# The first phase of a two-layer decoder trunk, issued in an order written by hand

## The chip, the cores and the metric

The kernel runs on one core of a Trainium2 chip. The metric is device time in microseconds (us) of one execution of the whole program. The kernel before was timed three times; one more execution was recorded by the hardware profiler, and every row below comes from that one.

## What is computed

The reference is a decoder trunk of two layers on 256 tokens of width 2048 in float32. In each layer a conditioning vector c gives shift, scale and gate vectors (the ada vectors), which modulate the input of a mixer and of a SwiGLU network. Layer 0 mixes with forgetting attention and, in parallel, an S5 state-space layer. Layer 1 has sliding-window attention. What matters here is the beginning of layer 0:

```python
mod = silu(c) @ w_ada[layer] + b_ada[layer]
sh1, sc1, g1, sh2, sc2, g2 = split(mod, 6)
h = x * (1 + sc1) + sh1
proj = h @ w_in          # q, k, v, forget logits f, and u, the input of S5
```

The S5 layer also needs parameters that depend on no token: powers of exp(lambda dt), sine and cosine tables, and products of these with the input and output matrices b and c.

## The kernel before

Everything is held transposed, with features on the 128 partitions and the 256 tokens along the free dimension. The width of 2048 makes 16 tiles of 128 features (`KT` = 16). A float32 weight tile is multiplied in three parts. `split` (lines 257 to 263) rounds a stretch of weights to a high half `wh` on ScalarE (the cast L261) and takes the rest as `wl` on VectorE (L262). The input is split likewise into `hi` and `lo`, side by side in `hp`. `mm3` (lines 602 to 605) then issues wh x hi (L603), wh x lo (L604) and wl x hi (L605), 256 columns each, for each tile of 128 x 128.

**The first phase** (lines 611 to 676) runs over the 16 input tiles k. For each k it computes the shift and scale of these 128 features, modulates x, and adds the products with 12 of the 32 output tiles of `w_in` (the 8 of u and 4 of k) into six PSUM banks. A step k has these parts:

- the *ada matmuls* L650: four pieces of `ada_s` against silu(c), 16 matmuls in the source and 32 records in the trace, into the bank `abank`;
- the copy of their partial sums to SBUF, L654 on ScalarE;
- two matmuls with `sel4` that add up these sums, L656 (four records);
- the *modulation*: L658 (adds the bias) and L660 (x times scale plus shift) on VectorE, L661 (`hi`) on ScalarE, L662 (`lo`) on VectorE;
- for each of two halves hf: `split` of 6 weight tiles, and the products, 18 matmuls.

Between these parts, `adv()` advances a generator, `s5_params` (lines 369 to 518), by one chunk up to its next `yield`. Its first five chunks are chains of VectorE instructions on 128 x 32 elements. Four chunks follow with three VectorE instructions on 128 x 512 (L460 to L464) and three ScalarE ones (L465 to L467), then eight chunks of three VectorE instructions (L475 to L481). Then, for each of four quarters, come two chunks of three VectorE instructions, the second with four ScalarE ones (L501), four groups of four transposes on TensorE (L506) each with a copy on ScalarE (L507), and 32 small matmuls into the bank `kc` (L514), whose copy (L518) opens the next chunk. Before, the four transpose groups of a quarter make two pieces. `make_crow` (lines 319 to 325) spreads silu(c) over the partitions, 8 matmul records in a call, four calls in steps 1 to 4.

**What sets the order.** The program is written once in Python, and a scheduler orders each engine's instructions as it finds them ready in its own timing, with dependences kept; each engine then runs its queue in that order. A few instructions are kept in their written order among themselves: the loads on SP, and the splits (`front`, lines 250 to 251).

**Transfers.** The weights come through a ring of `RING` = 9 tiles of 512 KB, on the queue of SP. Piece n + 9 can be issued when piece n was read (`release_piece`, lines 246 to 248). The pieces of the first phase are listed in the order in which they are sent (lines 614 to 618): four of ada_s and two of w_s (384 KB each) for each k. Three other loads are issued in the loop (`early`, line 622): the rest of the first half of x in step 0, the S5 arrays in step 1, the second half of x in step 4. `wh` and `wl` have three buffers each. After the phase, lines 677 to 696 compute the forget logits, finish the generator and copy the banks out; all other products follow from a planned stream of pieces.

Of the kernel before, what the change touches and what calls it, by code (L numbers as in the profile page):

```python
# [19 lines left out]
KT = D // 128  # L20
# [11 lines left out]
EK = (1, 4, 1, 2)  # L32
# [12 lines left out]
def _start_tiles():  # L45
    return [AB_U + i for i in range(8)] + [AB_K + i for i in range(4)]
# [219 lines left out]
def build(tc, I, out):  # L266
    nc = tc.nc
    V, A, PE, G = nc.vector, nc.scalar, nc.tensor, nc.gpsimd

    with ExitStack() as es:  # L270
        c = Ctx(tc, I, out, es)
# [47 lines left out]
        def make_crow(g):  # L319
            b = c.px.tile([128, 512], F32, tag="aux3", name=c.name("cr"))  # L320
            for i in range(4):
                k = 4 * g + i
                PE.matmul(b[:, 128 * i:128 * i + 128], lhsT=cs[:, k:k + 1].to_broadcast([128, 128]), rhs=ident,
                          start=True, stop=True, skip_group_check=True)
            A.copy(crow[:, 512 * g:512 * g + 512], b)
# [43 lines left out]
        def s5_params():  # L369
# [116 lines left out]
            for qd in range(4):  # L486
                H = slice(128 * qd, 128 * qd + 128)
                br, bi = (x[:, H].rearrange("p (a o h) -> p a o h", o=1, h=16).to_broadcast([128, 8, 4, 16]) for x in (b_re, b_im))
                wr, wi = (x[:, :, 8 * qd:8 * qd + 8].rearrange("p s (a o) -> p a s o", o=1).to_broadcast([128, 8, 4, 16])
                          for x in (wvr, wvi))  # L490
                e4 = [x.rearrange("p (a s h) -> p a s h", a=8, s=4) for x in (er, ei, w1, w2)]
                V.tensor_tensor(e4[0], br, wr, ALU.mult)
                V.tensor_tensor(e4[2], bi, wi, ALU.mult)
                V.tensor_tensor(er, er, w1, ALU.subtract)
                yield
                V.tensor_tensor(e4[1], bi, wr, ALU.mult)
                V.tensor_tensor(e4[3], br, wi, ALU.mult)
                V.tensor_tensor(ei, ei, w2, ALU.add)
                for cc, e in ((0, er), (1, ei)):
                    for g in range(2):  # L500
                        A.activation(eb[:, cc, :, g, :], a3(e), AF.Copy, scale=m2[:, g:g + 1])  # L501
                yield
                for aa in range(4):
                    b = c.px.tile([128, 512], F32, tag="aux3", name=c.name("tr"))
                    for n in range(4):
                        PE.transpose(b[:, 128 * n:128 * n + 128], ebf[:, n % 2, 2 * aa + n // 2, :], ident)  # L506
                    A.copy(el[qd][:, 512 * aa:512 * aa + 512], b)  # L507
                    if aa == 1:
                        yield
                b = c.px.tile([128, 512], F32, tag="aux3", name=c.name("kc"))  # L510
                for i in range(4):
                    for jj in range(2):
                        for cc in range(2):
                            PE.matmul(b[32 * i:32 * i + 32, 64 * jj:64 * jj + 64], lhsT=ebf[:, cc, 4 * jj + i, 96:128],  # L514
                                      rhs=gcv[cc][:, :, 8 * qd + 4 * jj + i, :], start=(cc == 0), stop=(cc == 1),
                                      skip_group_check=True, tile_position=(0, 32 * i))
                yield
                V.tensor_copy(kc[:, H], b[:, 0:128])  # L518
# [83 lines left out]
        def mm3(dst, wh, wl, P, k, first, last):  # L602
            PE.matmul(dst, lhsT=wh, rhs=hi_of(P, k), start=first, stop=False, skip_group_check=True)  # L603
            PE.matmul(dst, lhsT=wh, rhs=lo_of(P, k), start=False, stop=False, skip_group_check=True)  # L604
            PE.matmul(dst, lhsT=wl, rhs=hi_of(P, k), start=False, stop=last, skip_group_check=True)  # L605
# [5 lines left out]
        hp = pair_of(0, 1, 2, 3)  # L611

        n_st = len(_start_tiles())
        for k in range(KT):
            for q in range(4):
                c.add_piece(I["ada_s"][4 * k + q], 1024)
            for q in range(2):
                c.add_piece(I["w_s"][2 * k + q], 64 * n_st)
        stream_items = make_items(c, I)

        c.dma_to(RING - 1)
        early = {0: lambda: c.load(x_lo[:, 2 * T:], I["xT"][0][:, 2 * T:]), EK[0]: s5_load,
                 EK[1]: lambda: c.load(x_hi, I["xT"][1])}

        c.free_aux = deque()
        ubank = [c.acc() for _ in range(4)]
        kbank = [c.px.tile([128, 512], F32, tag=f"aux{i}", name=c.name("kb")) for i in range(2)]
        abank = c.px.tile([128, 512], F32, tag="aux2", name=c.name("ab"))
        ada0 = [scr[:, 256 * i:256 * i + 256] for i in range(2)]
# [8 lines left out]
        def adv():  # L638
            try:
                next(s5job)  # L640
            except StopIteration:
                pass

        for k in range(KT):
            early.get(k, lambda: None)()
            for q in range(4):
                t = c.ptiles[6 * k + q]
                for j in range(4):
                    kk = 4 * q + j
                    PE.matmul(abank[32 * j:32 * j + 32, 0:256], lhsT=cs[:, kk:kk + 32], rhs=t[:, 256 * j:256 * j + 256],  # L650
                              start=(q == 0), stop=(q == 3), skip_group_check=True, tile_position=(0, 32 * j))
                c.release_piece(6 * k + q)
            a = ada0[k % 2]
            A.copy(a, abank[:, 0:256])  # L654
            for v in range(2):
                PE.matmul(abank[:, 256 + 2 * k + v:257 + 2 * k + v], lhsT=a[:, 128 * v:128 * v + 128],  # L656
                          rhs=sel4, start=False, stop=True, skip_group_check=True)
            V.tensor_tensor(m0v[:, k, :], abank[:, 256 + 2 * k:258 + 2 * k], b0v[:, k, :], ALU.add)  # L658
            xt = xs[k // 8][:, k % 8, :]
            V.tensor_scalar(xt, xt, m0v[:, k, 1:2], m0v[:, k, 0:1], op0=ALU.mult, op1=ALU.add)  # L660
            A.copy(hi_of(hp, k), xt)  # L661
            V.tensor_sub(lo_of(hp, k), xt, hi_of(hp, k).bitcast(F32))  # L662
            for hf in range(2):
                hw = 64 * n_st
                wh, wl = c.split(c.ptiles[6 * k + 4 + hf][:, 0:hw], hw)
                c.release_piece(6 * k + 4 + hf)
                for i in range(n_st // 2):
                    s = hf * (n_st // 2) + i
                    bk = ubank[s // 2] if s < 8 else kbank[(s - 8) // 2]
                    o = bk[:, 256 * (s % 2):256 * (s % 2) + 256]  # L670
                    W = slice(128 * i, 128 * i + 128)
                    mm3(o, wh[:, W], wl[:, W], hp, k, k == 0 and s % 2 == 0, k == KT - 1)
            if EK[2] <= k < EK[2] + 4:
                make_crow(k - EK[2])
            for _ in range(EK[3]):
                adv()
        fbank = c.px.tile([128, 512], F32, tag="aux2", name=c.name("fb"))
        for k in range(KT):
# [968 lines left out]
```

## Time and profile before

| | |
|---|---|
| time, median of 3 runs | 2296.44 us (2294.65 to 2297.05) |
| the profiled execution | 2297.39 us |
| its span, first to last instruction | 2295.5 us |
| granted TensorE clock, mean | 0.989 of 2.4 GHz |
| TensorE matmuls (PE) busy | 2230.2 us, 97% |
| VectorE (DVE) busy | 1728.8 us, 75% |
| ScalarE (ACT) busy | 1133.3 us, 49% |
| HBM read | 576.55 MB, 252 GB/s over the span |

PE stands for TensorE's matmuls, PEld for its weight loads, which overlap them, DVE for VectorE, ACT for ScalarE and SP for the engine whose queue issues the weight transfers. A row of the timeline has the start and the duration in us, the engine, the source line, the operation, output <- input, and in brackets how long the engine stood idle before it and what ended that. A duration includes the tail of an instruction, which overlaps the next one; the distance between starts is the pace.

### The profile page before, as it was taken

Reading aid. Unit: us, or ns where it says so; the run is one execution under the profiler, and the core shown is the slowest. Engines: PE = TensorE matmul, PEld = TensorE weight load, DVE = VectorE, ACT = ScalarE, POOL = GpSimd, SP = SyncE. Lnnn points to the kernel's source line nnn. Section 1 sums busy time; section 2 is a strip of 40 time slices with the busy share of each in tenths; the row PEclk is TensorE's granted clock in tenths of the full one; section 3 lists DMA queues with packets and bytes.
Section 4 is the critical chain, followed back from the end, with each engine's and each line's share of the span. In section 5 each row is a group of like instructions: output and inputs, shape, how many; then the busy total and the mean of one; then the engine's idle time right before and its main releaser. Section 6 shows DMA issues by size and latency. Waiting matters only on the chain.

```text
span 2295.5 us, 38210 instructions
## 1 busy us (share of the span) xinstructions
PE 2230.2 (97%) x14702; PEld 1941.1 (85%) x14702; DVE 1728.8 (75%) x3062; ACT 1133.3 (49%) x1816; POOL 2.3 (0%) x6
## 2 busy tenths in 40 slices
PE   6999999999999999999999999999999999999996
PEld 4778887889888888888888988889888888888885
DVE  6648887888888888888887988687777555555576
ACT  3456565365444334444445665466444434444444
POOL 0000000000000000000000000000000000000000
PEclk9999999999999999999999999999999999999998
DMA  8998787948999999888875865357887666665662
GB/s 320 353 335 324 275 307 267 332 158 297 321 319 318 317 324 317 316 318 319 317 234 150 299 220 180 120 156 254 270 272 250 186 188 187 186 190 186 191 185 73
DMA packets 161479, 581.16 MB, mean 253 GB/s; under 512 B 18320, under 2 KB 18960, under 8 KB 160912
## 3 DMA queue, kind: packets, MB, share of 16 engines
q1 hardware_dynamic: 159984, 575.49, 73.4%
q10 hardware_dynamic: 1312, 3.23, 0.4%
q8 instruction: 115, 1.88, 0.3%
q14 instruction: 68, 0.56, 0.1%
HBM read 576.55 MB, written 2.10 MB: 252 GB/s over the span
## 4 chain that ended last, share of the span: by engine, by line
PE 95%; DVE 2%; ACT 1%; DMA 1%; issue 0%; ACTq 0%; DVEq 0%
PE acc L608 43%; PE acc L609 22%; PE acc L603 6%; PE acc L604 6%; PE acc L605 6%; PE acc L1291 2%; PE ab L650 1%; PE aux L556 1%; PE aux L727 1%; PE aux L1137 1%; PE aux L1125 0%; PE aux L1110 0%; PE aux L805 0%; PE aux L1109 0%; ACT wh L261 0%; DVE wl L262 0%
## 5 line engine op out<-in xcount | busy, mean ns | idle before, releaser
L608 PE MATMUL acc<-hp,wh 128*128 128x512 f32 x4288 | 1492.5, 397 | 3.6 <-DVE z L943 2.5
L609 PE MATMUL acc<-hp,wl 128*128 128x256 f32 x4288 | 1170.2, 280 | 0.5 <-DVE wl L262 0.5
L262 DVE TENSOR_TENSOR wl<-w,wh 128x1024 fp32r<-128x1024 f32 (+1 forms) x712 | 862.7, 1212 | 405.8 <-ACT wh L261 392.6
L261 ACT CAST wh<-w 128x1024 fp32r<-128x1024 f32 (+1 forms) x712 | 740.4, 1041 | 853.4 <-PE acc L608 459.5
L608 PEld LDWEIGHTS acc<-hp,wh 128*128 128x128 f32 x4288 | 792.8, 188 | 184.5 <-ACT lnb L963 2.8
L609 PEld LDWEIGHTS acc<-hp,wl 128*128 128x128 f32 x4288 | 808.8, 189 | 19.4 <-DVE wl L262 2.0
L534 DVE CUSTOM_DVE_ANT_0 w<-w,crow 128x1024 f32<-128x1024 f32 x280 | 341.1, 1220 | 0.0
L603 PE MATMUL acc<-hp,wh 128*128 128x256 f32 x1120 | 312.0, 294 | 19.9 <-ACT hp L1036 13.2
L604 PE MATMUL acc<-hp,wh 128*128 128x256 f32 x1120 | 318.9, 291 | 0.7 <-DVE hp L662 0.7
L605 PE MATMUL acc<-hp,wl 128*128 128x256 f32 x1120 | 303.4, 290 | 0.0
L603 PEld LDWEIGHTS acc<-hp,wh 128*128 128x128 f32 x1120 | 213.3, 196 | 36.5 <-ACT hp L1036 14.4
L604 PEld LDWEIGHTS acc<-hp,wh 128*128 128x128 f32 x1120 | 218.8, 195 | 8.1 <-issue 5.4
L605 PEld LDWEIGHTS acc<-hp,wl 128*128 128x128 f32 x1120 | 210.7, 195 | 3.4 <-issue 3.0
L943 DVE SCALAR_TENSOR_TENSOR z<-acc,mod,z 128x256 f32<-128x256 f32 x180 | 85.9, 482 | 37.0 <-PE acc L609 33.9
L1213 ACT COPY ftmp<-acc 128x256 f32<-128x256 f32 x80 | 29.8, 373 | 116.7 <-PE acc L609 116.7
L1214 DVE TENSOR_TENSOR ftmp<-acc,ftmp 128x256 f32<-128x256 f32 x80 | 33.9, 423 | 27.8 <-ACT ftmp L1213 27.8
L650 PE MATMUL ab<-w,cs 128*32 128x256 f32 x512 | 36.5, 403 | 14.9 <-ACT cs L315 11.7
L1291 PE MATMUL acc<-wh,hp 128*128 128x512 f32 (+1 forms) x192 | 47.5, 357 | 0.0
L1291 PEld LDWEIGHTS acc<-wh,hp 128*128 128x128 f32 x192 | 33.9, 189 | 5.8 <-issue 0.8
L1218 DVE TENSOR_TENSOR ftmp<-ftmp 128x256 f32<-128x256 f32 x80 | 33.9, 423 | 4.7
L650 PEld LDWEIGHTS ab<-w,cs 128*32 128x32 f32 x512 | 15.6, 113 | 25.3 <-ACT cs L315 11.7
L1225 DVE TENSOR_TENSOR hp<-ftmp,hp 128x256 fp32r<-128x256 f32 x88 | 36.6, 420 | 0.1
(302 smaller groups left out, 1451.8 us busy)
## 6 DMA issues: line engine op xcount, KB each, us to landing
w<-in_w_gu SPq DMA_DIRECT2D x352, 512.0 KB, 4.4
w<-in_ada SPq DMA_DIRECT2D x320, 512.0 KB, 4.9
w<-in_w_dn SPq DMA_DIRECT2D x176, 512.0 KB, 4.4
w<-in_ada_s SPq DMA_DIRECT2D x64, 512.0 KB, 6.2
w<-in_w_ab SPq DMA_DIRECT2D x40, 512.0 KB, 6.0
w<-in_w_c SPq DMA_DIRECT2D x40, 512.0 KB, 4.3
w<-in_w_oab SPq DMA_DIRECT2D x32, 512.0 KB, 5.0
w<-in_w_oc SPq DMA_DIRECT2D x32, 512.0 KB, 3.8
```

What stands on the lines that cost most here:

```text
L261: self.front(nc.scalar.copy(wh[:, :n], src), "act")
L262: self.front(nc.vector.tensor_sub(wl[:, :n], src, wh[:, :n].bitcast(F32)))
L534: c.front(V.tensor_tensor_reduce(t, t, crow[:, 1024 * half:1024 * half + 1024], scale=1.0, scalar=0.0, op0=ALU.mult, op1=ALU.add, accum_ou ...
L603: PE.matmul(dst, lhsT=wh, rhs=hi_of(P, k), start=first, stop=False, skip_group_check=True)
L604: PE.matmul(dst, lhsT=wh, rhs=lo_of(P, k), start=False, stop=False, skip_group_check=True)
L605: PE.matmul(dst, lhsT=wl, rhs=hi_of(P, k), start=False, stop=last, skip_group_check=True)
L608: PE.matmul(bank, lhsT=wh, rhs=both_of(P, k), start=first, stop=False, skip_group_check=True)
L609: PE.matmul(bank[:, 256:512], lhsT=wl, rhs=hi_of(P, k), start=False, stop=last, skip_group_check=True)
L650: PE.matmul(abank[32 * j:32 * j + 32, 0:256], lhsT=cs[:, kk:kk + 32], rhs=t[:, 256 * j:256 * j + 256], start=(q == 0), stop=(q == 3), skip ...
L943: ins = V.scalar_tensor_tensor(zt(L, t), src, L["g"][:, t:t + 1], zt(L, t), op0=ALU.mult, op1=ALU.add)
L1225: V.tensor_sub(lo_of(F["ap"], f), a, hi.bitcast(F32))
L1291: PE.matmul(dst, lhsT=act[:, X], rhs=ww[:, c0:c0 + w], start=first, stop=(last and act is lo), skip_group_check=True)
```

## The change

The first phase is put into a block (`tc.manual_schedule`) in which TensorE, VectorE and ScalarE each issue their instructions in the order in which the source writes them. The other queues, the order across engines, and the place of later work among them are left to the scheduler. The loop is written anew: the ada matmuls and the modulation of step k + 1 stand inside step k, between its two halves; `adv()` is called three times a step instead of twice, and `s5_params` yields after each of the four transpose groups. The pieces are listed in the order in which the new loop reads them: w of half 0, ada of the next k, w of half 1.

```diff
@@ s5_params
                     A.copy(el[qd][:, 512 * aa:512 * aa + 512], b)
-                    if aa == 1:
-                        yield
+                    yield
@@ build, the pieces
+        hw = 64 * n_st
+        ada_p, w_p = {}, {}
+
+        def ada_pieces_of(k):
+            for q in range(4):
+                ada_p[k, q] = c.add_piece(I["ada_s"][4 * k + q], 1024)
+
+        ada_pieces_of(0)
         for k in range(KT):
-            for q in range(4):
-                c.add_piece(I["ada_s"][4 * k + q], 1024)
-            for q in range(2):
-                c.add_piece(I["w_s"][2 * k + q], 64 * n_st)
+            w_p[k, 0] = c.add_piece(I["w_s"][2 * k], hw)
+            if k + 1 < KT:
+                ada_pieces_of(k + 1)
+            w_p[k, 1] = c.add_piece(I["w_s"][2 * k + 1], hw)
@@ build, the loop
-        for k in range(KT):
-            early.get(k, lambda: None)()
+        def ada_mms(k):
             for q in range(4):
-                t = c.ptiles[6 * k + q]
+                t = c.ptiles[ada_p[k, q]]
                 for j in range(4):
                     kk = 4 * q + j
                     PE.matmul(abank[32 * j:32 * j + 32, 0:256], lhsT=cs[:, kk:kk + 32], rhs=t[:, 256 * j:256 * j + 256],
                               start=(q == 0), stop=(q == 3), skip_group_check=True, tile_position=(0, 32 * j))
-                c.release_piece(6 * k + q)
+                c.release_piece(ada_p[k, q])
+            A.copy(ada0[k % 2], abank[:, 0:256])
+
+        def modulate(k):
             a = ada0[k % 2]
-            A.copy(a, abank[:, 0:256])
             for v in range(2):
                 PE.matmul(abank[:, 256 + 2 * k + v:257 + 2 * k + v], lhsT=a[:, 128 * v:128 * v + 128],
                           rhs=sel4, start=False, stop=True, skip_group_check=True)
...
             V.tensor_sub(lo_of(hp, k), xt, hi_of(hp, k).bitcast(F32))
-            for hf in range(2):
-                hw = 64 * n_st
-                wh, wl = c.split(c.ptiles[6 * k + 4 + hf][:, 0:hw], hw)
-                c.release_piece(6 * k + 4 + hf)
-                for i in range(n_st // 2):
...
-                    mm3(o, wh[:, W], wl[:, W], hp, k, k == 0 and s % 2 == 0, k == KT - 1)
-            if EK[2] <= k < EK[2] + 4:
-                make_crow(k - EK[2])
-            for _ in range(EK[3]):
+
+        def split_of_half(k, hf):
+            halves = c.split(c.ptiles[w_p[k, hf]][:, 0:hw], hw)
+            c.release_piece(w_p[k, hf])
+            return halves
+
+        def products(k, hf, wh, wl):
+            for i in range(n_st // 2):
...
+                mm3(o, wh[:, W], wl[:, W], hp, k, k == 0 and s % 2 == 0, k == KT - 1)
+
+        with tc.manual_schedule(engines={mybir.EngineType.PE, mybir.EngineType.DVE, mybir.EngineType.Activation}):
+            ada_mms(0)
+            modulate(0)
+            for k in range(KT):
+                early.get(k, lambda: None)()
+                products(k, 0, *split_of_half(k, 0))
+                adv()
+                if k + 1 < KT:
+                    ada_mms(k + 1)
+                if EK[2] <= k < EK[2] + 4:
+                    make_crow(k - EK[2])
+                adv()
+                if k + 1 < KT:
+                    modulate(k + 1)
+                products(k, 1, *split_of_half(k, 1))
                 adv()
```

## Rows read from the trace of the kernel before

**Rows 1.** The page: span, and busy time of each engine.

```profile
span 2295.5 us, 38210 instructions
PE 2230.2 (97%) x14702; PEld 1941.1 (85%) x14702; DVE 1728.8 (75%) x3062; ACT 1133.3 (49%) x1816; POOL 2.3 (0%) x6
```

**Rows 2.** Windows: stretch, length, busy us of PE, PEld, DVE, ACT, POOL; PEclk; DMA; GB/s.

```profile
11.00:60.00 49.00, 39.04 (x325) 29.11 (x326) 40.23 (x150) 20.59 (x39) 0.00 (x0) 0.90 0.87 329
31.40:38.20 6.80, 6.36 (x35) 5.24 (x32) 6.80 (x31) 2.96 (x6) 0.00 (x0) 0.50 0.97 382
48.50:51.90 3.40, 3.40 (x17) 3.16 (x16) 3.40 (x11) 1.48 (x4) 0.00 (x0) 0.50 0.97 344
60.00:164.00 104.00, 97.86 (x1053) 80.85 (x1052) 56.48 (x103) 47.85 (x85) 0.30 (x1) 1.00 0.92 340
```

**Rows 3.** Line L658: durations in ns, first and last start.

```profile
L658 DVE TENSOR_TENSOR mod<-ab,bad x16: 139/159/167, 19.2 to 160.3; 128x2 f32<-128x2 f32 x16
```

**Rows 4.** Timeline of PE: start, duration, line, operation.

```profile
11.74 1.93 PE L650 MATMUL ab<-w,cs 128*32 128x256 f32 x16 [11.74 <-ACT cs L315]
...
18.60 0.50 PE L656 MATMUL ab<-cst,scr 128*128 128x1 f32 x4
...
66.97 0.28 PE L604 MATMUL acc<-hp,wh 128*128 128x256 f32 x1
...
70.45 0.28 PE L605 MATMUL kb<-hp,wl 128*128 128x256 f32 x1
...
72.58 0.66 PE L506 MATMUL tr<-cst,ebd 128*128 128x128 f32 x4 [0.19 <-ACT el L507]
...
74.70 1.93 PE L650 MATMUL ab<-w,cs 128*32 128x256 f32 x32
...
168.69 0.28 PE L605 MATMUL kb<-hp,wl 128*128 128x256 f32 x1
```

**Rows 5.** Waits from 0 to 300 us: total, times, longest.

```profile
ACT wh L261 <- PE acc L604: 32.9, 17, 3.5
```

**Rows 6.** The chain from 0 to 300 us: start, length, what.

```profile
160.67 1.23 PE kc L514 x29
```

**Rows 7.** Timeline of DVE.

```profile
12.48 0.18 DVE L379 TENSOR_SCALAR scr<-ebd 128x32 f32<-128x32 f32 x1 [8.31 <-DMA ebd<-in_s5p]
...
13.59 0.18 DVE L384 TENSOR_SCALAR scr<-scr 128x32 f32<-128x32 f32 x1
...
19.21 0.16 DVE L658 TENSOR_TENSOR mod<-ab,bad 128x2 f32<-128x2 f32 x1 [0.99 <-PE ab L656]
...
67.19 0.70 DVE L498 TENSOR_TENSOR et<-et 128x512 f32<-128x512 f32 x1
67.79 0.70 DVE L494 TENSOR_TENSOR et<-et 128x512 f32<-128x512 f32 x1
...
79.94 0.96 DVE L262 TENSOR_TENSOR wl<-w,wh 128x768 fp32r<-128x768 f32 x1 [1.66 <-ACT wh L261]
...
81.73 0.41 DVE L660 TENSOR_SCALAR x<-x,mod 128x256 f32<-128x256 f32 x1
```

**Rows 8.** Timeline of ACT.

```profile
31.47 0.40 ACT L661 CAST hp<-x 128x256 fp32r<-128x256 f32 x1
31.77 0.73 ACT L467 ACTIVATE cos<-cos,hpe 128x512 f32<-128x512 f32 x1
...
41.06 0.37 ACT L654 COPY scr<-ab 128x256 f32<-128x256 f32 x1 [4.09 <-PE ab L650]
...
67.93 2.57 ACT L501 ACTIVATE ebd<-et,cst 128x512 f32<-128x512 f32 x4 [2.29 <-DVE et L498]
...
71.94 0.59 ACT L507 COPY el<-tr 128x512 f32<-128x512 f32 x1
...
79.07 0.83 ACT L261 CAST wh<-w 128x768 fp32r<-128x768 f32 x1 [1.51 <-issue]
```

**Rows 9.** DMA issues from 0 to 300 us: count, KB each, median us to landing.

```profile
w<-in_ada_s SPq DMA_DIRECT2D x64, 512.0 KB, 6.2
```

More of the change, by code (lines that the diff above doesn't have):

```diff
@@ L662, in build @@
             V.tensor_sub(lo_of(hp, k), xt, hi_of(hp, k).bitcast(F32))
-            for hf in range(2):
-                hw = 64 * n_st
-                wh, wl = c.split(c.ptiles[6 * k + 4 + hf][:, 0:hw], hw)
-                c.release_piece(6 * k + 4 + hf)
-                for i in range(n_st // 2):
[L668 to L671, printed above, removed]
-                    mm3(o, wh[:, W], wl[:, W], hp, k, k == 0 and s % 2 == 0, k == KT - 1)
-            if EK[2] <= k < EK[2] + 4:
-                make_crow(k - EK[2])
-            for _ in range(EK[3]):
+        def split_of_half(k, hf):
[4 more added lines that the diff above has]
+            for i in range(n_st // 2):
+                s = hf * (n_st // 2) + i
+                bk = ubank[s // 2] if s < 8 else kbank[(s - 8) // 2]
+                o = bk[:, 256 * (s % 2):256 * (s % 2) + 256]
+                W = slice(128 * i, 128 * i + 128)
+                mm3(o, wh[:, W], wl[:, W], hp, k, k == 0 and s % 2 == 0, k == KT - 1)
[14 more added lines that the diff above has]
+                products(k, 1, *split_of_half(k, 1))
                 adv()
```

## The prediction

> **What bounds it now.** I read the page first: TensorE is busy in 97% of a span of 2295.5 us [rows 1], so every stretch in which it waits or runs slowly is worth its full length, and nothing else is. The change touches one stretch only, the sixteen steps of the first phase, so the windows come next [rows 2]. From 11 to 60 us TensorE is busy in 39.0 of 49 us, and its clock was granted at half, 1.2 GHz, in two pieces of it, 6.8 and 3.4 us long. From 60 to 164 us it is busy in 97.9 of 104 us at 2.4 GHz. The sixteen modulations L658 begin between 19.2 and 160.3 us [rows 3], 9.4 us apart on average, and the last product of the phase starts at 168.69 and ends at 168.9 us [rows 4]. So some 10 us of waits and 5 of slow clock lie before 60 us, 6 us after. That is all that a perfect order could win, about 20 us.
>
> How does the order of before reach 94% after 60 us? By running ahead. The cast L261 waited 17 times for a product two or three halves back to free a `wh` buffer (32.9 us in all) [rows 5]: the split of a half was made long before TensorE came to it, and the ScalarE and VectorE work of the S5 job was put wherever these engines were free. Which instruction goes where was the scheduler's choice.
>
> **What the change does, step by step.** In the new block each of the three engines issues in the order written. The code gives, for step k: split (k,0), products (k,0), S5 chunk, ada matmuls of k+1 with the copy of their sums, S5 chunk, modulation of k+1, split (k,1), products (k,1), S5 chunk. No engine gets more work; the extra `yield`s only cut the S5 job into 45 chunks for 48 calls. What changes is who waits behind whom, so I follow the chain.
>
> *Pieces.* The 18 matmuls of a half start 0.12 us apart (30 starts from 66.97 to 70.45), 2.16 us; the ada matmuls of a step take 1.93 us, a group of four transposes 0.55 (0.66 with its tail), the L656 group 0.50 [rows 4]; the 32 kc matmuls 1.23 [rows 6].
>
> *Turn A, modulation before split (k,1).* L656 to L658 takes 0.61 us (18.60 to 19.21) [rows 4, 7]; L658 0.20 and L660 0.45 with their hand-overs of 0.04 [rows 7]; the next ScalarE instruction begins 0.30 after L661 begins; the cast L261 is 0.83 and 0.04 to its reader (79.07 to 79.94) [rows 7, 8]. First matmul of half 1: 2.43 us after L656 began, of which TensorE works 0.5. Each tile needs `wl` at its third matmul, and L262 only starts when the cast ends: 1.0 us more [rows 7], less the first two matmuls. Then 16 matmuls and a tail, 2.1. From L656 to the end of the half: 5.5 us, 2.7 of them work. Before, the two casts had been done earlier; now they stand behind L661 on ScalarE, and L262 behind L662 on VectorE.
>
> *Turn B, an S5 chunk at the end of the step.* If it is a transpose chunk, the copy L507 (0.59) must wait for TensorE to finish products (k,1) and the transposes, and the cast of (k+1,0) is queued behind that copy: 0.05 + 0.59 + 0.04 + 0.87 + 1.0 + 2.1 = 4.6 us to the end of products (k+1,0) instead of 2.2 [rows 7, 8].
>
> *Steps 6 to 14.* A step with three transpose chunks: 0.55 + 1.93 + 0.55 + 5.5 + 0.55 + 4.6 = 13.7 us. Steps 9 and 11 are such. Steps 6 and 13 have no transposes in the first place: 13.1. Steps 7 and 14 end on kc matmuls, which hold up no cast: 0.55 + 1.93 + 0.55 + 5.5 + 1.23 + 2.2 = 12.0. In step 8 the four L501 (2.57) stand between L654 (0.4) and L661 [rows 8]: 1.93 + 0.4 + 2.6 + 4.2 (L661 to the end of the half) + 0.55 + 4.6 = 14.3. In step 10 two of them, behind three VectorE instructions, hold up the cast of step 11: 1.23 + 1.93 + 0.4, then 2.4 + 1.0 + 1.9 + 1.3 + 0.9 + 1.0 + 2.1 = 14.2. In step 12 only VectorE work lies there: 0.55 + 1.93 + 1.23 + 8.7 = 12.4. Sum of the nine: 118.5.
>
> *Steps 0 to 5.* Here VectorE's parameter chunks set the pace, as L658 of the next step is queued behind them. Dependent 32-wide instructions go 0.22 us apart (six starts from 12.48 to 13.59) [rows 7]. Before, two chains ran interleaved. Step 0 has 35 of them ahead of L658, 7.7 us, and 7 more with three ScalarE ones between the splits: 14.5 us. Step 1 has 53, partly independent, some 6.9 us, then three 512-wide VectorE (0.60 apart, 67.19 to 67.79) [rows 7] and three ScalarE instructions like L467 (0.73) [rows 8] ahead of the cast: 15.5. Step 2 has such a trio twice, 15.5. Steps 3 and 4 have 1.9 us of VectorE between the two L262, and a crow (two groups like the transposes, 1.1): 11.5 each; step 5 10.8. Sum 79.3.
>
> *Start and sum.* Ada matmuls of step 0 run cold, 16 in 1.93 us against 32 later [rows 4], so 3.87 from 11.74; copy 0.42, turn A 5.5: products (0,0) end at 21.5. 21.5 + 79.3 + 118.5 + 2.2 for the last half = 221.5 us, against 168.9: **52.6 us longer at full clock.**
>
> *The clock.* TensorE would work 8.4 us of 13.7 in a late step, 61%, and wait in four places of 0.7 to 1.9 us. Between 11 and 60 us it worked 80% of the time and had 10.2 of 49 us, 21%, at 1.2 GHz [rows 2]. Lower end: no loss at all. Upper end: every matmul of the nine late steps and half of the early work at half clock, 9 x 8.4 + 12 = 88 us. I take the share that the row shows, 21% of 210 us = 44 us, busy to about three quarters, half of it lost: 17 us. It is the nearest row, and the pieces of before ended after 3.4 and 6.8 us of dense products, so the clock should come back in each step.
>
> *The transfers.* A step needs 4 x 512 + 2 x 384 KB, 2.88 MB; over 13 us that is 222 GB/s against 340 moved between 60 and 164 us [rows 2]. Nine ring pieces cover a step and a half, some 19 us, and a piece lands in 6.2 us [rows 9]. So the new order of the transfers is worth 0 here; if that cover went (steps of 8 us), a piece that comes too late would cost at most its landing, 6 us, once. The three moved loads on SP (rest of x, S5 arrays, second half of x) stand behind the ring's issues as before and are read a step or more later.
>
> *After the phase* nothing is edited; the later phases, and with them their 97%, move as a block.
>
> The profiled execution took 2297.4 us, 0.9 above the median of 2296.44. 2297.4 + 52.6 + 17 = **2367 us**.
>
> **Rivals.**
> - *The clock stays at 2.4 GHz.* For it: after the dense products the clock came back each time [rows 2]. Against: 61% busy is less than what lost it before. Time: 2297.4 + 52.6 = 2350.
> - *The clock falls in every step and most work is cold.* Four waits in each step, for nine steps, speak for it; the recovery in dense products against it. Time: 2297.4 + 52.6 + 88 = 2438. The Trainium skill, "TensorE: Matmul & The Clock Gate", section "HAM oscillation", has this as a rule: a loop whose bursts of matmuls are parted by long enough waits starts each burst at the half clock, again and again. By that rule this rival would be the likeliest; the rows show the fall, but twice only, not a loop that stays in it.
> - *Faster: the queues hold no one up.* If the splits are in fact ready when TensorE reaches them (the point that decides: L261 of (k,1) ends before L656 of k+1 does), each step costs its work alone: 4.3 + 1.93 + 0.5 + 0.9 of S5 on average = 7.6 us. With 18.5 to the first product (11.74 + 3.87 + 0.42 + 2.43) and 4.4 for the crows that is 18.5 + 16 x 7.6 + 4.4 = 144.5, 24 us less; at the 340 GB/s of the row a step is 8.5 us and 18.5 + 16 x 8.5 = 154.5, 14 less. In between: 2278. For it: the steps after 60 us come close to that pace. Against: the written order puts that cast after L661, which cannot start before L656 ends.
> - *The block doesn't bind,* the order comes out as before: 2297. Against: the block names the three engines.
> - *A part only:* hand-overs shorter and chunks better covered than I count, half of the 52.6: 2324.
>
> **Chances.** Forecast 0.55, clock full 0.26, cold 0.07, faster 0.06, as before 0.02, a part 0.04. The range 2330 to 2405 holds the forecast and the full clock, 0.81; its low end leaves 20 us for overlaps that I missed at full clock, its high end is half clock for over half of the phase (105 us x 3/4 / 2 = 39, 2389) and 16 us of longer waits. Leaving out 0.12 below and 0.07 above. Slower by over 0.2% (4.6 us, what a measurement of this kernel can tell from no change): 0.92; within it 0.02; faster 0.06.
>
> **What would show it.** Right, if L658 starts about 13 us apart in the later steps and the last one lies past 200 us; if the waits list TensorE on L261 and on L262 about once for each half (16 x 0.7 to 1.9 us), and L261 no longer on old products; if the windows between 100 and 200 us show TensorE busy in some 12 of 20 us, granted clock under 1, and DMA near 220 GB/s; and if everything behind the phase is as long as before. Wrong, if TensorE stays above 90% there (then the casts were ready), or if the extra time lies behind the phase.

## The result, and the profile after

The changed kernel takes **2375.37 us**, median of 4 runs (2372.59 to 2377.91), against 2295.93 of the kernel before in the same comparison (2294.65 to 2297.05). The ratio is 1.0342, 95% interval 1.0327 to 1.0358: 79 us slower. The prediction was 2367 us in a range of 2330 to 2405.

The page of the changed kernel; the first two lines answer to [rows 1], the third is the granted clock in 40 slices of the span.

```profile
span 2374.6 us, 38206 instructions
...
PE 2269.1 (96%) x14702; PEld 1976.9 (83%) x14702; DVE 1735.9 (73%) x3062; ACT 1134.6 (48%) x1817; POOL 2.3 (0%) x6
...
PEclk8787999999999999999999999999999999999998
```

TensorE is busy 39 us longer than in [rows 1] with as many instructions, and the span is 79 us longer. The clock was below 2.4 GHz in the first four slices, 59 us each, and hardly anywhere else: what happened, happened in the first phase. Windows of the changed kernel; columns as in [rows 2].

```profile
140.00:160.00 20.00, 15.51 (x101) 13.54 (x102) 3.03 (x6) 4.00 (x7) 0.00 (x0) 0.76 0.57 190
160.00:180.00 20.00, 14.25 (x120) 11.86 (x119) 7.95 (x13) 6.12 (x10) 0.00 (x0) 0.82 0.48 149
11.00:243.90 232.90, 178.71 (x1420) 146.23 (x1421) 103.83 (x253) 75.85 (x137) 0.30 (x1) 0.82 0.65 225
```

In the five windows of 20 us between 100 and 200 us, of which two are shown, TensorE is busy in 13.9 to 15.7 us, where it had 97.9 of 104 [rows 2], at a mean clock of 0.76 to 0.91, and the transfers move 149 to 227 GB/s instead of 340. The line of the modulation's first instruction, L666, answers to [rows 3]:

```profile
L666 DVE TENSOR_TENSOR mod<-ab,bad x16: 153/159/160, 17.1 to 231.4; 128x2 f32<-128x2 f32 x16
```

The last of the sixteen begins at 231.4 us, not 160.3. What TensorE waited for meanwhile, in the waits of the changed kernel from 11 to 244 us (total, times, longest):

```profile
ACT scr L659 <- PE ab L656: 59.8, 16, 8.9
ACT el L507 <- PE tr L506: 51.1, 16, 5.7
...
PE acc L602 <- ACT wh L261: 41.3, 23, 3.2
...
PE acc L604 <- DVE wl L262: 9.2, 24, 0.5
```

TensorE waits 23 times for a cast of weights to `wh` (L261) and 24 times for a `wl` (L262), 50.5 us together. ScalarE waits in turn for TensorE's transposes and ada matmuls: these two engines hand work to and fro and wait by turns. One late step in the timeline of PE, ACT and DVE shows how; ahead of 155.65 is the turn at the modulation, and from 159.86 on the turn behind a transpose chunk:

```profile
153.10 0.61 PE L664 MATMUL ab<-cst,scr 128*128 128x1 f32 x4
...
153.82 0.16 DVE L666 TENSOR_TENSOR mod<-ab,bad 128x2 f32<-128x2 f32 x1 [7.25 <-ACT el L507]
...
154.46 0.40 ACT L669 CAST hp<-x 128x256 fp32r<-128x256 f32 x1 [0.64 <-DVE x L668]
154.77 0.83 ACT L261 CAST wh<-w 128x768 fp32r<-128x768 f32 x1
...
155.65 0.39 PE L602 MATMUL acc<-hp,wh 128*128 128x256 f32 x1 [1.94 <-ACT wh L261]
...
156.64 0.39 PE L604 MATMUL acc<-hp,wl 128*128 128x256 f32 x1 [0.49 <-DVE wl L262]
...
156.98 0.31 PE L603 MATMUL acc<-hp,wh 128*128 128x256 f32 x1
...
157.10 0.40 PE L604 MATMUL acc<-hp,wl 128*128 128x256 f32 x1
...
157.30 0.41 PE L602 MATMUL kb<-hp,wh 128*128 128x256 f32 x1
...
157.52 0.41 PE L603 MATMUL kb<-hp,wh 128*128 128x256 f32 x1
...
159.86 0.92 PE L506 MATMUL tr<-cst,ebd 128*128 128x128 f32 x4
160.82 0.58 ACT L507 COPY el<-tr 128x512 f32<-128x512 f32 x1 [5.22 <-PE tr L506]
161.30 0.83 ACT L261 CAST wh<-w 128x768 fp32r<-128x768 f32 x1
...
162.19 0.39 PE L602 MATMUL acc<-hp,wh 128*128 128x256 f32 x1 [1.41 <-ACT wh L261]
...
163.18 0.38 PE L604 MATMUL acc<-hp,wl 128*128 128x256 f32 x1 [0.49 <-DVE wl L262]
```

The cast of 154.77 waits for nothing of its own: it begins when the cast L669 lets it, which stands ahead of it in ScalarE's queue and waits for the modulation. The cast of 161.30 stands behind the copy L507, which waited 5.22 us for the transposes of 159.86. (The row of L666 names the copy L507. But L666 begins 0.11 us after L664 ends, at 153.71, as it does where the row names L664, so I read it as waiting for L664.) Beside this one sees the clock, which was granted at 2.4 GHz up to 157.1 us and at 1.2 GHz behind it: the products start 0.12 us apart from 156.98 to 157.10 and 0.21 from 157.30 on, in the middle of dense work.

The last product of the phase and three others, timeline of PE (the last of half 0 in steps 0, 6 and 15, then of the phase):

```profile
23.28 0.41 PE L604 MATMUL acc<-hp,wl 128*128 128x256 f32 x1
...
104.82 0.28 PE L604 MATMUL acc<-hp,wl 128*128 128x256 f32 x1
...
239.84 0.28 PE L604 MATMUL acc<-hp,wl 128*128 128x256 f32 x1
...
243.57 0.28 PE L604 MATMUL kb<-hp,wl 128*128 128x256 f32 x1
```

The phase ends at 243.85 us, 74.9 later than the 168.97 of [rows 4]; the rest of the span, 2130.8 us, is 4.2 longer than before (2126.5).

### The profile page after: what moved, and what is told of

It reads as the page before. It is cut to its first block, busy times and chain, and to the rows that moved or that the text cites. A ratio compares the mean times of both kernels' runs of the same rounds, so it can differ in the third digit from the quotient of the medians.

```text
span 2374.6 us, 38206 instructions
## 1 busy us (share of the span) xinstructions
PE 2269.1 (96%) x14702; PEld 1976.9 (83%) x14702; DVE 1735.9 (73%) x3062; ACT 1134.6 (48%) x1817; POOL 2.3 (0%) x6
## 4 chain that ended last, share of the span: by engine, by line
PE 92%; DVE 4%; ACT 3%; DMA 1%; issue 1%; ACTq 0%; DVEq 0%
PE acc L607 42%; PE acc L608 21%; PE acc L604 6%; PE acc L602 6%; PE acc L603 6%; PE acc L1315 2%; DVE wl L262 1%; PE ab L656 1%; ACT wh L261 1%; PE aux L555 1%; PE aux L751 1%; PE aux L1161 0%; PE aux L1149 0%; PE aux L1134 0%; PE aux L1133 0%
## 5 line engine op out<-in xcount | busy, mean ns | idle before, releaser
L262 DVE TENSOR_TENSOR wl<-w,wh 128x1024 fp32r<-128x1024 f32 (+1 forms) x712 | 862.8, 1213 | 412.6 <-ACT wh L261 396.5
L261 ACT CAST wh<-w 128x1024 fp32r<-128x1024 f32 (+1 forms) x712 | 739.1, 1040 | 815.2 <-PE acc L607 470.6
L607 PEld LDWEIGHTS acc<-hp,wh 128*128 128x128 f32 x4288 | 792.9, 188 | 185.7 <-issue 3.4
L602 PE MATMUL acc<-hp,wh 128*128 128x256 f32 x1120 | 326.7, 301 | 54.5 <-ACT wh L261 41.3
L603 PE MATMUL acc<-hp,wh 128*128 128x256 f32 x1120 | 326.1, 297 | 0.0
L602 PEld LDWEIGHTS acc<-hp,wh 128*128 128x128 f32 x1120 | 223.0, 201 | 68.3 <-ACT wh L261 46.4
L603 PEld LDWEIGHTS acc<-hp,wh 128*128 128x128 f32 x1120 | 225.9, 202 | 4.0 <-issue 3.7
L666 DVE TENSOR_TENSOR mod<-ab,bad 128x2 f32<-128x2 f32 x16 | 2.5, 159 | 69.4 <-ACT el L507 36.2
```

Of the source, the lines that this page charges most:

```text
L261: self.front(nc.scalar.copy(wh[:, :n], src), "act")
L262: self.front(nc.vector.tensor_sub(wl[:, :n], src, wh[:, :n].bitcast(F32)))
L607: PE.matmul(bank, lhsT=wh, rhs=both_of(P, k), start=first, stop=False, skip_group_check=True)
```

## The experiments

The theory: ScalarE's written order puts the cast of a half's weights behind an eviction or a modulation that waits for TensorE, and so makes TensorE wait for it in two places of each step (turn A at the modulation, turn B behind a transpose chunk); VectorE's parameter chunks set the pace of the first steps; the clock falls as a consequence. Rivals: TensorE's own new order, the order of the transfers, or the clock as the main cost. The phase's end is that of its last product in the profiled execution, the rest is that execution's span behind it. How much later work TensorE has drawn in ahead of that product differs from kernel to kernel, by some 4 us at the most (an estimate from 1378 to 1418 matmul records, the fillers apart), so small differences of the phase's end show little. Each ratio is to the runs of before in the same comparison, whose medians were 2295.48 to 2296.89 us.

| kernel | time, us (runs) | ratio to before, 95% | phase's end | rest of the span |
|---|---|---|---|---|
| before | 2295.93 (4) | 1 | 168.97 | 2126.5 |
| changed | 2375.37 (4) | 1.0342 [1.0327, 1.0358] | 243.85 | 2130.8 |
| no block | 2304.59 (5) | 1.0040 [1.0026, 1.0054] | 161.63 | 2141.2 |
| TensorE's order only | 2309.82 (4) | 1.0067 [1.0052, 1.0083] | 170.47 | 2137.6 |
| TensorE's and ScalarE's | 2367.27 (4) | 1.0307 [1.0289, 1.0325] | 236.37 | 2129.6 |
| split of half 1 early | 2346.51 (4) | 1.0220 [1.0205, 1.0235] | 201.10 | 2145.4 |
| split of half 0 early | 2341.19 (4) | 1.0199 [1.0180, 1.0218] | 211.59 | 2124.5 |
| both splits early | 2319.48 (4) | 1.0096 [1.0079, 1.0113] | 186.30 | 2132.5 |
| S5 job outside | 2342.88 (4) | 1.0207 [1.0192, 1.0223] | 211.35 | 2127.4 |
| both early, S5 outside | 2292.81 (10) | 0.9988 [0.9978, 0.9997] | 161.68 | 2126.8 |
| both early, S5 behind | 2335.15 (4) | 1.0178 [1.0161, 1.0195] | 197.54 | 2132.9 |
| filling matmuls | 2365.41 (4) | 1.0309 [1.0293, 1.0324] | 227.74 | 2134.0 |
| before, new pieces | 2303.76 (4) | 1.0038 [1.0023, 1.0053] | 162.33 | 2141.0 |
| changed, old pieces | 2374.40 (4) | 1.0339 [1.0318, 1.0360] | 236.54 | 2128.6 |

### Whose order costs the time

**No block.** The new source text in the scheduler's order.

```diff
-        with tc.manual_schedule(engines={PE, DVE, Activation}):
+        if True:
```

> The rewritten loop, the finer yields and the new order of transfers stay; only the block that fixes the order of the three engines is gone, so the scheduler places instructions again. Theory (the fixed order costs the time): the casts run ahead again and the time is that of the kernel before within 10 us, 2286 to 2306. Rival (the rewriting or the transfers cost it): the time stays above 2340.

2304.59 us. So 71 of the 79 us hang on the block. The phase itself is 7.3 us shorter than before; the rest of the span is 14.7 us longer, though nothing in it was edited: the scheduler ordered the later work otherwise (TensorE's matmuls behind the phase stand in another order than before).

**TensorE's order only, then TensorE's and ScalarE's.** Here and below, the diffs leave out lines that only carry a name along.

```diff
-        with tc.manual_schedule(engines={PE, DVE, Activation}):
+        with tc.manual_schedule(engines={PE}):
```

> The changed kernel with the order kept by TensorE alone; ScalarE and VectorE get their instructions in the scheduler's order. If TensorE waits because the block also fixes where the casts of the blocks' weights stand on ScalarE and VectorE (behind the evictions and the modulation of the same step), the casts run ahead again and most of the loss goes: 2290 to 2315 us. If it is TensorE's own order, with products right behind the split that they need, the time stays above 2340 us.

2309.82 us: the first range. The waits of this kernel from 11 to 244 us, and one step of its ScalarE timeline:

```profile
ACT wh L261 <- DMA w<-in_w_s: 21.4, 15, 4.2
...
PE acc L602 <- ACT wh L261: 0.9, 1, 0.9
```

```profile
132.62 0.83 ACT L261 CAST wh<-w 128x768 fp32r<-128x768 f32 x1 [0.42 <-DMA w<-in_w_s]
133.50 0.38 ACT L659 COPY scr<-ab 128x256 f32<-128x256 f32 x1
134.06 0.59 ACT L507 COPY el<-tr 128x512 f32<-128x512 f32 x1 [0.18 <-PE tr L506]
135.29 0.41 ACT L669 CAST hp<-x 128x256 fp32r<-128x256 f32 x1 [0.64 <-DVE x L668]
```

With ScalarE free the cast of 132.62 stands ahead of the copy L659, the eviction L507 and the modulation L669. By the written order of the changed kernel a cast of half 1 comes behind the step's L659 and L669. TensorE waits once for a `wh`, 0.9 us, against 41.3; the casts now wait for the transfers (21.4 us). TensorE's own order is nearly harmless: the phase ends 8.8 us later than with no block, and the time is 5 us longer.

```diff
-        with tc.manual_schedule(engines={PE, DVE, Activation}):
+        with tc.manual_schedule(engines={PE, Activation}):
```

> The changed kernel with the order kept by TensorE and ScalarE; VectorE gets its instructions in the scheduler's order. If ScalarE's order, which sets the cast to the high part behind the eviction of the same step, is what makes TensorE wait (41.3 us of waits for the high parts against 9.2 us for the low parts), the time stays above 2345 us. If VectorE's order (parameter chunks ahead of the modulations, the low parts behind them) carries as much, 2310 to 2340 us.

2367.27 us, the first case: adding ScalarE's order to TensorE's costs 57 us, and adding VectorE's to both only 8 more. That holds for this order of adding; VectorE's order without ScalarE's was not run. TensorE's wait for `wh` is back in full (its waits, 11 to 240 us):

```profile
PE acc L602 <- ACT wh L261: 41.7, 20, 3.9
PE acc L604 <- DVE wl L262: 12.9, 21, 1.7
```

### Which places in that order

**The split of half 1 early** takes turn A away: the casts of (k,1) are written behind those of (k,0). The weight pieces come in the order of before, so that they are there.

```diff
...
-                products(k, 0, *split_of_half(k, 0))
+                h0 = split_of_half(k, 0)
+                h1 = split_of_half(k, 1)
+                products(k, 0, *h0)
...
-                products(k, 1, *split_of_half(k, 1))
+                products(k, 1, *h1)
```

> Block kept; the split of (k,1) is written right behind the split of (k,0), and its piece is sent right behind that of (k,0). This takes turn A away: the products of half 1 no longer wait for the modulation of k+1. Theory: about 1.9 us of wait and 0.5 of wait for wl in each of 15 steps, some 36 us, and about half of the 37 us that the half clock costs: 2315 to 2340. Rival (it is the S5 chunks that hold the engines up, not the place of the split): above 2360.

2346.51 us, 29 less than the changed kernel, but 7 above the range. The phase ends 42.8 us earlier; 14.6 of these are lost again behind the phase.

**The split of half 0 early** takes turn B away: the casts of (k+1,0) are written behind those of (k,1), ahead of the last chunk of step k.

```diff
...
-                products(k, 1, *split_of_half(k, 1))
+                h1 = split_of_half(k, 1)
+                if k + 1 < KT:
+                    h0 = split_of_half(k + 1, 0)
+                products(k, 1, *h1)
```

> Block kept; the split of (k+1,0) is written right behind the split of (k,1), ahead of the last S5 chunk. This takes turn B away. Theory: about 2 us in each of the seven late steps that end on a transpose or ScalarE chunk and 1 to 3 us in the early ones, 25 us together, and a share of the clock: 2330 to 2350. Rival (turn B is covered by something else): above 2365.

2341.19 us, in the range, 34 less than the changed kernel.

**Both early**: (k+1,0) is split behind the ada matmuls of k+1, (k+1,1) behind its modulation, and each is used a half step or more later. Here, and in the two kernels built on it, the pieces come in the order of before.

```diff
...
                     ada_mms(k + 1)
+                    h0 = split_of_half(k + 1, 0)
...
                     modulate(k + 1)
+                    n1 = split_of_half(k + 1, 1)
-                products(k, 1, *split_of_half(k, 1))
+                products(k, 1, *h1)
+                h1 = n1
```

> Block kept; both splits of k+1 are written before the products of (k,1), half a step to a step ahead of their use, with the pieces in the order in which they are read. Takes both turns away. Theory: most of the 38 us of waits and of the 37 us of slow clock go, and only the first steps, where VectorE's parameter chunks lie ahead of the modulation, are slower than before: 2275 to 2310. Rival (a fixed order cannot keep TensorE busy whatever the place of the splits): above 2330.

2319.48 us: 56 less, and still 10 above the range. Its waits of TensorE from 11 to 240 us say what was missed:

```profile
PE acc L602 <- ACT hp L672: 16.3, 7, 3.6
...
PE acc L602 <- ACT wh L261: 2.6, 2, 1.9
```

The waits for `wh` are gone (2.6 us). TensorE now waits for the modulated x (L672), five of the seven times in steps 1 to 5, where the parameter chunks stand ahead of the modulation on VectorE. Its transposes wait 6.9 us more, in five places, for ScalarE's L501. That is a third place, of the S5 job and not of the splits.

### The S5 job

**S5 job outside**: the three `adv()` of a step are taken out, and the whole generator runs in the loop that finishes it, behind the block in the source; the scheduler places its work.

```diff
                 products(k, 0, *split_of_half(k, 0))
-                adv()
                 if k + 1 < KT:
                     ada_mms(k + 1)
...
-                adv()
                 if k + 1 < KT:
                     modulate(k + 1)
                 products(k, 1, *split_of_half(k, 1))
-                adv()
```

> The changed kernel with the whole S5 job written behind the block, so that the scheduler places it among the ordered instructions. Turn A stays, turn B is gone, and no parameter chunk stands ahead of a modulation. Theory: a step is 1.9 + 0.4 + 5.5 + 2.2 = 10 us, 16 x 10 + 18 + some 5 to 10 us of S5 work that finds no gap, and 10 to 15 us of slow clock: 2315 to 2345. Rival (the S5 chunks are not what waits): above 2360.

2342.88 us, in the range: 32 less than the changed kernel, with turn A still there.

**Both early, S5 outside**: the two edits together.

> Both splits early, as in e4_both_early, and the S5 job behind the block, as in e6_s5_outside. In e4_both_early TensorE waits 16 us for the cast of hi, which stands behind VectorE's parameter chunks and ScalarE's S5 work, and 7 us for the input of transposes; these go. Theory: steps of 8 to 8.5 us, the phase ends between 155 and 165 us: 2280 to 2298, as fast as the kernel before or a little faster. Rival (the S5 work then lands behind the phase and delays it there): above 2305.

2292.81 us, in the range and 0.9988 of before. The 56 and 32 us of the two parts come out nearly whole together: 83 of 88. Two windows of it:

```profile
60.00:100.00 40.00, 36.90 (x393) 31.15 (x395) 23.56 (x42) 19.36 (x34) 0.00 (x0) 1.00 0.93 344
100.00:140.00 40.00, 39.32 (x438) 33.63 (x431) 17.11 (x33) 20.63 (x37) 0.30 (x1) 1.00 0.97 347
```

TensorE is busy in 76 of 80 us from 60 to 140, at full clock. The phase ends 7.3 us earlier than before; the median is 2.7 us below the 2295.48 of before in the same comparison. The interval lies below 1, but the gain is under the 0.2% that I count as told apart. It is the best of the kernels tried, and says that a written order need not cost: the two places and the S5 job hold the whole loss.

**Both early, S5 behind.** If the chunks hurt only by standing ahead of a modulation, moving them behind it should do as much.

```diff
-                adv()
+                if k >= 3:
+                    adv()
...
-                adv()
                 if k + 1 < KT:
                     modulate(k + 1)
                     n1 = split_of_half(k + 1, 1)
+                adv()
```

> The kernel with both splits drawn one place ahead (2319.5 us), with the chunks of the parameters' transposition moved within the order: the first only from step 3 on, the second behind the modulation and the split of half 1 instead of ahead of them. If what is left of the loss there is VectorE's parameter chunks standing ahead of a modulation in the first steps, 2285 to 2310 us. If the chunks cost TensorE the same wherever they stand in the order, 2315 us or more.

2335.15 us: slower than with the chunks in place, so the first reading fell. TensorE's waits from 11 to 240 us, and ScalarE's timeline ahead of the longest:

```profile
PE ab L667 <- ACT scr L662: 19.6, 14, 6.9
...
PE acc L602 <- ACT hp L672: 5.6, 4, 2.6
```

```profile
55.59 0.63 ACT L465 ACTIVATE sin<-et 128x512 f32<-128x512 f32 x1 [6.66 <-DVE et L464]
...
59.87 0.72 ACT L467 ACTIVATE cos<-cos,hpe 128x512 f32<-128x512 f32 x1
60.49 0.35 ACT L662 COPY scr<-ab 128x256 f32<-128x256 f32 x1
```

The wait for L672 shrank from 16.3 to 5.6 us, as meant, but the sum of the ada partials (L667) now waits 14 times for its copy L662, 19.6 us against 4.0 with both splits early. Behind the moved chunk the copy stands after L465, which waited 6.66 us for VectorE's chain; and with no chunk between ada matmuls and L667, TensorE has nothing to do while the copy runs. I read the chunk as having been a cover; a run that moves the second chunk alone, without holding back the first, was not made. Among the three kernels with both splits early, the chunk cost time at either fixed place, and only leaving its place free (the kernel above) cost nothing.

### The clock

**Filling matmuls**: 12 matmuls of 128 columns into unused columns of `abank` behind each modulation and 8 behind the last chunk of a step, to keep TensorE at work in both turns.

```diff
                     modulate(k + 1)
+                    fill(12)
                 products(k, 1, *split_of_half(k, 1))
                 adv()
+                if k + 1 < KT and k not in (7, 14):
+                    fill(8)
```

> The changed kernel with work added: in each step 12 matmuls of 128 columns (ident by ident into a part of abank that nobody reads) behind the modulation, and 8 behind the last S5 chunk, where TensorE waits for a cast. No wait is taken away. Theory (half of the added time is the half clock that these waits bring, some 37 us): the clock stays at 2.4 GHz for most of the phase and the time falls although there is more to do, to 2340 to 2360. Rival (waits alone cost the time, the slow clock only fills them): 2375 or more.

2365.41 us: faster by 10 us with 568 more matmul records, but short of the expected 15 to 35. Its windows, and the products that answer to those shown of the changed kernel:

```profile
11.00:60.00 49.00, 42.14 (x372) 35.30 (x373) 30.63 (x127) 15.34 (x31) 0.00 (x0) 1.00 0.83 296
...
100.00:140.00 40.00, 37.80 (x381) 33.34 (x380) 13.27 (x26) 13.81 (x25) 0.00 (x0) 1.00 0.66 218
```

```profile
22.68 0.41 PE L603 MATMUL acc<-hp,wh 128*128 128x256 f32 x1
22.90 0.35 PE L604 MATMUL acc<-hp,wl 128*128 128x256 f32 x1
...
102.96 0.28 PE L604 MATMUL acc<-hp,wl 128*128 128x256 f32 x1
...
224.12 0.28 PE L604 MATMUL acc<-hp,wl 128*128 128x256 f32 x1
...
227.46 0.28 PE L604 MATMUL kb<-hp,wl 128*128 128x256 f32 x1
```

The granted clock is 1.00 throughout by this view, and the phase ends 16.1 us earlier than in the changed kernel. (Up to 22.90 us the products go 0.21 to 0.22 us apart all the same, as where 1.2 GHz was granted above, so there the view is not to be trusted.)

The 16.1 us are not the whole price of the clock, because the fillers (L674) take time of their own. Rows of this kernel, from a turn at the modulation and from a turn without a wait:

```profile
163.06 0.96 DVE L262 TENSOR_TENSOR wl<-w,wh 128x768 fp32r<-128x768 f32 x1 [0.31 <-ACT wh L261]
...
164.47 0.29 PE L604 MATMUL acc<-hp,wl 128*128 128x256 f32 x1
...
194.41 1.95 PE L674 MATMUL ab<-cst 128*128 128x128 f32 x16
196.11 0.36 PE L602 MATMUL acc<-hp,wh 128*128 128x256 f32 x1
```

The `wl` is ready at 164.02, and its first reader begins 0.45 us later, since the fillers held up the two products ahead of it. In the changed kernel that distance is 0.05 us (163.13 to 163.18). It is so in twelve of the fifteen turns at the modulation, 0.41 us too much each, 4.9 us together. Behind steps 3, 4, 5 and 12 the casts are ready in both kernels, so there is no wait to fill, and the eight fillers stand between two halves for 1.7 us each time (194.41 to 196.11), 6.8 together. So some 12 of the 58.8 us by which this phase is longer than before are the fillers' own. What is left is an estimate: about 47 us for the waits at full clock, and 16.1 + 12, about 28 us, for the clock in the changed kernel. It is good to some 3 us, as it compares two single executions, one 1.1 us above its kernel's median, the other 2.0 below.

### The transfers

**The kernel before with the new order of pieces**, then **the changed kernel with the old one**.

```diff
-            for q in range(4):
-                c.add_piece(I["ada_s"][4 * k + q], 1024)
-            for q in range(2):
-                c.add_piece(I["w_s"][2 * k + q], 64 * n_st)
+            w_p[k, 0] = c.add_piece(I["w_s"][2 * k], hw)
+            if k + 1 < KT:
+                ada_pieces_of(k + 1)
+            w_p[k, 1] = c.add_piece(I["w_s"][2 * k + 1], hw)
```

> The kernel before with nothing but the new order of the pieces in the ring (w of half 0, ada of the next k, w of half 1). Theory (the order of the transfers is worth nothing): 2290 to 2302, within 0.3% of before. Rival (it is a part of the loss, as the old loop reads the pieces in another order): 2305 or more.

2303.76 us, between the two ranges and nearer to the rival's, but not for its reason: the phase ends 6.6 us *earlier*, and the rest of the span is 14.5 us longer. Counting matmul records (the n-th need not be the same matmul in both), the kernel is 7.9 us ahead of before at the 1300th, 2.8 ahead at the 2300th, 2.7 behind at the 3600th and 6.4 at the 11600th. The loss is made in several places of later work, which stands in another order than before. Why it did so I did not try.

```diff
-            w_p[k, 0] = c.add_piece(I["w_s"][2 * k], hw)
...
             if k + 1 < KT:
                 ada_pieces_of(k + 1)
-            w_p[k, 1] = c.add_piece(I["w_s"][2 * k + 1], hw)
+                for hf in range(2):
+                    w_p[k + 1, hf] = c.add_piece(I["w_s"][2 * k + 2 + hf], hw)
```

> The changed kernel with the transfers in the order of before (a step's conditioning piece, then both of its weight pieces). If the order of the transfers is worth nothing beside the order of the engines, as the prediction took it, 2369 to 2381 us. If the new order of the transfers is worth some us in the phase, as it was in the kernel before (6.6 to 7.9 us earlier at the phase's end), 2380 to 2386 us; if it costs, 2368 us or less.

2374.40 us, in the middle of the first range: 1 us from the changed kernel, with intervals that overlap nearly whole. (Its profiled execution was the shortest of its four, 2366.86 us at a mean clock of 0.977; the others took 2374.22 or more at 0.970 to 0.973. So its phase's end in the table is an early one.) Where the engines wait for each other, the order of the transfers is worth nothing that can be measured.

## Why the prediction was right

**What bounds and whose order.** The forecast blamed casts that can no longer run ahead on ScalarE. With TensorE's order alone the time is 2309.82, with ScalarE's added 2367.27; that step is shown. The sharper form, 57 us with ScalarE's queue and 8 more with VectorE's, was not in it.

**Turns A and B.** From L664 to the first product the forecast had 2.43 us; in the step shown it is 155.65 - 153.10 = 2.55, with waits of 1.94 and 0.49. Turn B shows 1.41 and 0.49. The waits for the cast are of the size of the "0.7 to 1.9" that the prediction named, those for `wl` a little under it. L261 was to wait no longer for old products [rows 5]. Of the 17 waits in that row only 8 (19.7 us) lie within the first phase, up to 169 us; in the changed kernel none does, up to 244 us.

**The step lengths.** The ends of half 0 in steps 0, 6 and 15 cut the phase where the sum was cut:

| stretch | predicted, full clock | filling matmuls | changed |
|---|---|---|---|
| to the end of products (0,0) | 21.5 | 23.25 | 23.69 |
| steps 0 to 5 | 79.3 | 79.99 | 81.41 |
| steps 6 to 14 | 118.5 | 121.16 | 135.02 |
| last half | 2.2 | 3.34 | 3.73 |
| phase's end | 221.5 | 227.74 | 243.85 |

The middle column still holds the fillers' own time, some 6.7 us in steps 0 to 5 and 5.0 in steps 6 to 14. Without it the nine late steps take about 116 us, 12.9 each where 13.2 were predicted, and the early ones about 73 where 79.3 were. So the full-clock term of 52.6 us was too high, by some 5.5 us, and most of that lies in the early steps. The start was 1.8 us too short (the first products ran at the pace of 1.2 GHz, 0.21 us apart), and the last half 1.1, where the forget logits and later work are drawn in between. The early steps were priced by VectorE's chunks, but in the changed kernel L666 follows them without a wait only at 27.14 and 40.48 us; from then on it waits for TensorE's sums:

```profile
55.43 0.16 DVE L666 TENSOR_TENSOR mod<-ab,bad 128x2 f32<-128x2 f32 x1 [1.86 <-PE ab L664]
```

In the changed kernel L666 comes 15.4 us apart from step 7 on (108.17 to 231.44, eight steps), not 13. With the fillers, and their own time, it comes 13.6 us apart; the difference is the clock.

**The clock: too small, and hidden in the sum.** The term was 17 us, and the estimate above is about 28. The step that failed is the share of time at 1.2 GHz, taken as 21% from [rows 2]. The window from 11 to 243.9 us has a mean of 0.82, so (1 - 0.82) x 2 = 36% or 84 us instead of 44. By the prediction's own formula these cost 84 x 3/4 / 2 = 31 us, close to the 28. Of these some 8 lie in steps 0 to 5 (81.41 - 79.99 and the 6.7 of the fillers), some 19 in steps 6 to 14 (135.02 - 121.16 and 5.0). The Trainium skill, "TensorE: Matmul & The Clock Gate", section "HAM oscillation", counts half of a throttled stretch as lost; by that 84 us would cost 42. The Trainium skill also has each burst of matmuls behind a long enough wait start at the half clock. In the step shown, behind waits of 1.94 and 0.49 us, the burst starts fast (0.12 us apart) and slows at 157.1 within dense products. That the clock falls again and again, in most steps, agrees with the Trainium skill here, and the rival built on it was right in the fall and wrong in the price: it had 88 us of loss.

**The transfers at 0.** Right for this kernel (1 us, old pieces). The reason given, slack in the ring, is only half the story: where the casts run ahead, as in the kernel before, the same reordering ends the phase 6.6 us earlier, and the casts wait for transfers (21.4 us with TensorE's order alone).

**Behind the phase nothing changes.** Off by 4.2 us, 0.2%. Counted by matmul records, 5.0 us are lost close behind the phase (73.7 us behind before at the 1450th, 78.7 at the 1500th), where TensorE waits 1.73 us for a copy of `kT` at 253.13 and the clock is at 1.2 GHz from 252.7 to 259.5. By the 2300th 3.5 of them are won back, and by the 3600th lost again; there one wait for a piece is seen in the timeline of PE:

```profile
476.41 1.05 PE L555 MATMUL aux<-w,cs 128*32 128x512 f32 x4 [2.30 <-DMA w<-in_ada]
```

In the sum: 2297.4 + 47 + 28 + 4.2 = 2376.6, against the 2376.43 of the profiled execution. The prediction had 52.6 + 17 + 0 and fell 9.4 us short of that execution (8.4 of the median): some 11 too little for the clock and 4.2 behind the phase, less some 5.5 too much at full clock. The mechanism was right; that the number came so close is in part luck, since errors of opposite sign cut a miss of some 15 us to 9.

**Signs named ahead.** Last L666 past 200 us, TensorE's waits on L261 and L262 (23 and 24 times in 32 halves), and transfers near 220 GB/s (225 over the phase): seen. TensorE busy "some 12 of 20 us" was not: it is 13.9 to 15.7, and slow matmuls count as busy for longer.

## What to carry to other kernels

A software pipeline fixes an order on every engine that takes part, and each engine then waits at its own queue's head, as ScalarE did here. Before fixing an order, look for work that ran ahead in the old one (here the casts, seen as waits for a free buffer), and write it at least as far ahead of its use; the engine that both prepares inputs and evicts outputs is the one to check. Fixing TensorE's order cost 5 us here (2304.59 to 2309.82), and fixing ScalarE's on top of it 57. Side work that has no deadline is better left to a scheduler than given a fixed place: it was worth 32 us in the changed kernel and 27 more beside early splits.

## What was not expected of the hardware and the scheduler

More matmuls made the kernel faster: 568 more records took 10 us off (1.0309 [1.0293, 1.0324] against 1.0342 [1.0327, 1.0358]), since TensorE kept 2.4 GHz from 23 us to the phase's end, and although the fillers took some 12 us of their own. The clock fell in the middle of dense products, shortly after waits of 1.94 and 0.49 us, not at the start of a burst. And an edit in the first phase moved the rest of the span, untouched in the source, by up to 19 us (2126.5 us before, 2145.4 with the split of half 1 early); where in the scheduler's choices that begins stays open.
